# Sums of weight blocks in the second MLP matmul: accumulating DMAs onto a negated copy in place of VectorE subtractions

## The chip, the cores and the metric

The kernel runs on one core of one Trainium2 chip. The metric is the device time of one execution in microseconds. The kernel before took 1455.29 us (median of 3 runs, 1454.57 to 1456.90). Engines are named as in the profile: PE is TensorE, PEld its weight loads, DVE VectorE, ACT ScalarE, POOL GpSimd, SP SyncE. PE, DVE, ACT, POOL and SP each work through a queue of their own in order, and semaphores join them.

## The reference

A two-layer encoder trunk on a sequence of 512 tokens of width 1024, in float32. Layer 0 mixes tokens with dilated window attention, layer 1 with latent attention; after each mixer comes an MLP. The part that matters here is the MLP:

```python
D_MODEL = 1024; SEQ = 512; DEPTH = 2; D_FF = 4 * D_MODEL
def sq_relu_mlp(h, w1, w2):
    a = jax.nn.relu(h @ w1)
    return (a * a) @ w2
...
        h = rms_norm(x, norm_ffn[i])
        x = x + sq_relu_mlp(h, ffn_w1[i], ffn_w2[i])
```

## The kernel before

Every matmul keeps float32 accuracy by splitting both operands in a high and a low part (type fp32r) and adding three products: high x high, high x low, low x high. For weights the split is two instructions: ACT copies the block into a tile `whi`, then DVE subtracts that from the block into `wlo`. Both tile names have four buffers that all weight splits of the kernel use in turn, so a split can run ahead of PE by four half blocks and no more; ACT waits until PE has freed the buffer.

The MLP works through the 4096 hidden columns in four chunks. `up(ch, 0)` and `up(ch, 1)` compute the hidden activations of a chunk with `run_block` (matmuls on line 184, results `acc`, evacuated by ACT on lines 604 and 605). `down` multiplies a chunk by 1024 rows of `w2`, for the first three chunks of each MLP (six times in the program) by `wino`, and for the last chunk by `run_block`. The order is up, up, then for each chunk: up(next, 0), down, up(next, 1).

`wino` is a Strassen-Winograd product on 2 x 2 blocks: seven block products in place of eight. The activations and `w2` are cut in four blocks each; a weight block is two half blocks of 128 partitions x 1024 float32 (512 KB each). The four weight blocks b11, b12, b22, b21 lie in `wqs`, loaded by SP (line 505). The products run in the order 1, 5, 6, 3, 7, 2, 4, 24 matmuls each (line 571), into PSUM tiles `sc` and `tp`, and are added to `resid` on line 553. Their weight operands are, in this order:

- 1: b11
- 5: b12 - b11, written over b11
- 6: b22 minus that, written over b11
- 3: b22
- 7: b22 - b12, written over b12
- 2: b21
- 4: b21 minus the sum of 6, written over b11

`sub` makes these four sums, on line 513, two half blocks each; `split_w` splits each operand into `whi` (line 523) and `wlo` (line 524). A half block may be overwritten by the next sum only when its split is done. `stmp` and `split_a` do the same for the activations (tiles `S` and `asp`).

The program is recorded in the order of the code, and a scheduler then sets the order of each engine's queue by a simulated timeline. It decides where a sum stands relative to the splits and the evacuations.

Of the kernel before, what the change touches and what calls it, by code (L numbers as in the profile page):

```python
# [10 lines left out]
F32 = mybir.dt.float32  # L11
F32R = mybir.dt.float32r
AF = mybir.ActivationFunctionType
ALU = mybir.AluOpType
# [5 lines left out]
NT = S // P  # L20
# [67 lines left out]
def encoder_kernel(ctx: ExitStack, tc: tile.TileContext, x, norm_mix, norm_ffn, a_w_qkv, a_q_gain, a_k_gain,  # L88
                   a_w_o, b_w_in, b_q_a_gain, b_w_qb, b_kv_a_gain, b_w_kvb, b_q_gain, b_k_gain, b_w_o,
                   ffn_w1, ffn_w2, consts, out):  # L90
    nc = tc.nc
    V, A, G, PE = nc.vector, nc.scalar, nc.gpsimd, nc.tensor
    uid = [0]

    def nm(s):
        uid[0] += 1
        return f"{s}_{uid[0]}"
# [42 lines left out]
    def load_raw(src, nk, dims, n):  # L140
        raw = wp.tile([P, 2, 512], F32, tag="raw", name=nm("raw"), bufs=3)
        dst = raw[:, :nk, :n]
        if dims:
            dst = dst.rearrange("p k (t c) -> p k t c", t=dims)
            for k in range(nk):
                nc.sync.dma_start(dst[:, k], src[:, k])
        else:
            nc.sync.dma_start(dst, src)
        return raw

    def load_unit(src, nk, dims, n, key=None, home=None):

        raw = early.pop(key) if key in early else load_raw(src, nk, dims, n)
        if home is None:
            home = [wp.tile([P, 2, 512], F32R, tag=t, name=nm(t)) for t in ("whi", "wlo")]
        hi, lo = home
        A.activation(hi[:, :nk, :n], raw[:, :nk, :n], AF.Copy)  # L157
        V.tensor_tensor(lo[:, :nk, :n], raw[:, :nk, :n], hi[:, :nk, :n].bitcast(F32), op=ALU.subtract)  # L158
        return hi, lo, nk

    def run_block(units, groups, n, mm, evac, outs=NT, name=None, halves=1):

        accs = [acc_p.tile([P, 512], F32, tag="acc", name=nm("acc")) for _ in range(outs)]
        total = sum(u[1] for u in units)
        ui = 0
        kt0 = 0  # L170
        for gi, g in enumerate(groups):
            loaded = []
            for _ in range(g):
                src, nk, dims = units[ui]
                loaded.append(load_unit(src, nk, dims, n, (name, ui)))
                ui += 1
            nkt = 0
            for hv in range(halves):
                for o in range(outs):
                    kt = kt0  # L180
                    for hi, lo, nk in loaded:
                        for j in range(nk):
                            for p_i, (lt, rt, oc) in enumerate(mm(o, kt, hi[:, j], lo[:, j], hv)):
                                PE.matmul(accs[o][:, oc], lhsT=lt, rhs=rt, start=(kt == 0 and p_i == 0 and hv == 0),  # L184
                                          stop=(kt == total - 1 and p_i == 2), skip_group_check=halves > 1)
                            kt += 1
                    nkt = kt
                    if gi == len(groups) - 1 and hv == halves - 1:
                        evac(o, accs[o])
            kt0 = nkt  # L190
# [10 lines left out]
    def w_units(w, n0, n):  # L201

        v = w.rearrange("(k p) c -> p k c", p=P)
        return [(v[:, k:k + 2, n0:n0 + n], 2, None) for k in range(0, v.shape[1], 2)]
# [278 lines left out]
    def split_a(x, pool):  # L483
        t = pool.tile([P, 4, 2, 256], F32R, tag="asp", name=nm("asp"), bufs=4)
        A.activation(t[:, :, 0], x, AF.Copy)
        V.tensor_tensor(t[:, :, 1], x, t[:, :, 0].bitcast(F32), op=ALU.subtract)
        return t

    def wino(tag, Aq, w, wqs, pool, resid):

        v = w.rearrange("(k p) c -> p k c", p=P)
        raw, S = {}, {}

        def load(key, slot):
            ki, ni = key  # L500
            raw[key] = []
            for u in range(2):
                t = wqs[:, 2 * slot + u]
                k0 = 4 * ki + 2 * u
                nc.sync.dma_start(t, v[:, k0:k0 + 2, 512 * ni:512 * ni + 512])
                raw[key].append(t)
        for key, slot in zip(((0, 0), (0, 1), (1, 1), (1, 0)), SLOTS[tag % 2]):
            load(key, slot)
        b11, b12, b22, b21 = raw[0, 0], raw[0, 1], raw[1, 1], raw[1, 0]

        def sub(o, x, y):
            for u in range(2):
                V.tensor_tensor(o[u], x[u], y[u], op=ALU.subtract)  # L513

        def stmp(name, x, y, op):
            if name not in S:
                S[name] = pool.tile([P, 4, 256], F32, tag="S", name=nm("S"), bufs=2)
            V.tensor_tensor(S[name], x, y, op=op)

        def split_w(x):  # L520
            hi = wp.tile([P, 2, 512], F32R, tag="whi", name=nm("whi"))
            lo = wp.tile([P, 2, 512], F32R, tag="wlo", name=nm("wlo"))
            A.activation(hi, x, AF.Copy)  # L523
            V.tensor_tensor(lo, x, hi.bitcast(F32), op=ALU.subtract)  # L524
            return hi, lo

        def operands(p):
            if p == 1:
                return Aq(0, 0), b11
            if p == 5:  # L530
                stmp("c", Aq(1, 0), Aq(1, 1), ALU.add)
                sub(b11, b12, b11)
                return S["c"], b11
            if p == 6:
                stmp("c", S["c"], Aq(0, 0), ALU.subtract)
                sub(b11, b22, b11)
                return S["c"], b11
            if p == 3:
                stmp("c", Aq(0, 1), S["c"], ALU.subtract)
                return S["c"], b22  # L540
            if p == 7:
                stmp("d", Aq(0, 0), Aq(1, 0), ALU.subtract)
                sub(b12, b22, b12)
                return S["d"], b12
            if p == 2:
                return Aq(0, 1), b21
            sub(b11, b21, b11)
            return Aq(1, 1), b11

        def add_to(i, n, banks):  # L550
            for t in range(2):
                sl = resid[:, 2 * i + t, 512 * n:512 * n + 512]
                V.tensor_tensor(sl, sl, banks[t], op=ALU.add)

        banks = {}
        for p, chain, first, adds in ORDER:
            a, wq = operands(p)
            at = split_a(a, pool)
            if first:
                pl, tg = (sc_p, "sc") if chain == "a" else (tp_p, "tp")  # L560
                banks[chain] = [pl.tile([P, 512], F32, tag=tg, name=nm(tg)) for _ in range(2)]
            bk = banks[chain]
            for u in range(2):
                hi, lo = split_w(wq[u])
                for t in range(2):
                    for j in range(2):
                        k = 2 * u + j
                        ah = at[:, k, 0, t * P:(t + 1) * P]
                        al = at[:, k, 1, t * P:(t + 1) * P]
                        for i, (lt, rt) in enumerate(((ah, hi), (ah, lo), (al, hi))):  # L570
                            PE.matmul(bk[t], lhsT=lt, rhs=rt[:, j], start=(first and k == 0 and i == 0),  # L571
                                      stop=(k == 3 and i == 2), skip_group_check=True)
            for i, n in adds:
                add_to(i, n, bk)
# [6 lines left out]
    def mlp(layer, w1, w2, hT_m, resid, pool, done):  # L581
# [4 lines left out]
        def up(ch, grp):  # L586
            if grp == 0:
                if ch % 2:
                    a2s[ch] = pool.tile([P, 8, S], F32, tag="a2", name=nm("a2"))
                else:  # L590
                    a2s[ch] = x16.tile([P, 8, S], F32, tag="x16", name=nm("a2"))
            a2 = a2s[ch]
            c0 = ch * 1024 + grp * 512
            first = c0 == 0

            def mm(o, kt, hi, lo, hv, n=256 if first else 512):
                wh, wl = hi[:, o * P:(o + 1) * P], lo[:, o * P:(o + 1) * P]
                sl = slice(hv * n, hv * n + n)
                hh, hl = hT_m[:, kt, 0, sl], hT_m[:, kt, 1, sl]
                return [(wh, hh, sl), (wh, hl, sl), (wl, hh, sl)]  # L600

            def evac(o, acc):
                f = grp * 4 + o
                A.activation(a2[:, f], acc, AF.Relu)
                A.activation(a2[:, f], a2[:, f], AF.Square)

            run_block(w_units(w1, c0, 512), [4] if first else [1] * 4, 512, mm, evac, halves=2 if first else 1)

        def down(ch):
            a2 = a2s.pop(ch)  # L610
# [3 lines left out]
        def down_last(ch):  # L614
# [13 lines left out]
            for c in range(2):  # L628
                def evac(r, acc, c=c):
# [4 lines left out]
                          mm, evac)  # L634

        up(0, 0)
        up(0, 1)
        for ch in range(3):
            up(ch + 1, 0)
# [316 lines left out]
```

## Time and profile before

| | |
|---|---|
| median of 3 runs | 1455.29 us |
| the profiled execution | 1457.98 us |
| its span, first to last instruction | 1456.2 us |
| granted TensorE clock | 0.995 |
| busy PE / DVE / ACT / POOL | 1422.8 / 903.5 / 710.3 / 117.4 us |
| `sub` on DVE (line 513) | 48 instructions, 58.0 us |
| moved by DMA | 135.58 MB, 93 GB/s mean |

The rows of the profile that the prediction uses stand there. "Busy" is the time in which an engine ran an instruction; a group's row ends in the idle time just before its instructions and what ended it. In a timeline a row is start, duration, engine, line, operation, output<-input and, in brackets, the idle time before it with its releaser. Start times count from the first instruction of the span. A matmul row shows its whole latency, so rows overlap; from one start to the next it is 0.227 us for 128x512.

### The profile page before, as it was taken

The page shows a single profiled execution, that of the slowest core. Times are in us where ns is not written, and L with a number is a line of the kernel's source. Part 1 is how long each engine was busy: PE and PEld are TensorE (multiplying, and loading weights), DVE is VectorE, ACT ScalarE, POOL GpSimd, SP SyncE. Part 2 cuts the span into 40 slices and gives each one's busy share as a digit, 9 for nine tenths or more (in the row PEclk, how much of TensorE's full clock was granted, in tenths as well). Part 3 has the DMA queues.
Part 4 walks back from the last instruction along what each step waited for, and adds up shares of the span by engine and source line. Part 5 has one row for each costly group of instructions (what it writes and reads, how often), then busy time and mean ns, then how long its engine had stood idle before and what let it go on. Part 6 is the DMA issues. An engine that isn't in the chain of part 4 may idle for free.

```text
span 1456.2 us, 19181 instructions
## 1 busy us (share of the span) xinstructions
PE 1422.8 (98%) x7164; PEld 1210.6 (83%) x7164; DVE 903.5 (62%) x1431; ACT 710.3 (49%) x1572; POOL 117.4 (8%) x133
## 2 busy tenths in 40 slices
PE   7999999999999999999999999999999999999998
PEld 6889889889988878888888888776778888888887
DVE  6765466556437655285776835688754286675832
ACT  5544455355335533553644543787633453544530
POOL 1120120011011100000000010322100000000000
PEclk9999999999999999999999999999999999999999
DMA  6325114322531334415151032300014305151031
GB/s 227 102 55 167 59 46 131 102 63 58 171 94 58 95 130 157 147 36 171 40 174 58 15 111 68 97 30 30 30 44 162 127 30 173 44 172 61 7 111 72
DMA packets 113053, 135.58 MB, mean 93 GB/s; under 512 B 7488, under 2 KB 72256, under 8 KB 112960
## 3 DMA queue, kind: packets, MB, share of 16 engines
q1 hardware_dynamic: 112960, 134.35, 29.5%
q8 instruction: 57, 0.93, 0.3%
q14 instruction: 36, 0.29, 0.1%
HBM read 130.13 MB, written 4.19 MB: 92 GB/s over the span
## 4 chain that ended last, share of the span: by engine, by line
PE 94%; ACT 3%; DVE 2%; issue 1%; DMA 0%; POOL 0%; SPq 0%; DVEq 0%; ACTq 0%
PE acc L184 64%; PE sc L571 9%; PE tp L571 7%; PE tp L123 4%; PE acc L867 1%; PE sc L761 1%; PE acc L843 1%; PE sco L440 1%; PE sco L444 1%; PE sc L351 1%; PE sc L843 1%; DVE wlo L158 1%; PE sc L344 0%; PE tp L867 0%; PE sc L340 0%
## 5 line engine op out<-in xcount | busy, mean ns | idle before, releaser
L184 PE MATMUL acc<-whi,hT 128*128 128x512 f32 (+2 forms) x1600 | 486.5, 379 | 5.5 <-DVE t L311 2.2
L158 DVE TENSOR_TENSOR wlo<-raw,whi 128x1024 fp32r<-128x1024 f32 (+3 forms) x186 | 215.3, 1162 | 297.5 <-ACT whi L157 296.5
L157 ACT ACTIVATE whi<-raw 128x1024 fp32r<-128x1024 f32 (+3 forms) x186 | 187.2, 1010 | 317.8 <-PE acc L184 256.6
L184 PEld LDWEIGHTS acc<-whi,hT 128*128 128x128 f32 x1600 | 296.3, 189 | 47.1 <-issue 2.9
L184 PE MATMUL acc<-hT_f,whi 128*128 128x512 f32 (+1 forms) x1152 | 322.7, 367 | 1.7 <-DVE resid L650 1.2
L184 PE MATMUL acc<-wlo,hT 128*128 128x512 f32 (+2 forms) x800 | 299.9, 375 | 0.0
L184 PEld LDWEIGHTS acc<-hT_f,whi 128*128 128x128 f32 x1152 | 209.1, 189 | 37.4 <-DVE resid L650 1.6
L184 PE MATMUL acc<-hT_f,wlo 128*128 128x512 f32 (+1 forms) x576 | 208.3, 366 | 0.0
L184 PEld LDWEIGHTS acc<-wlo,hT 128*128 128x128 f32 x800 | 151.3, 189 | 19.9 <-DVE wlo L158 0.5
L523 ACT ACTIVATE whi<-wqs 128x1024 fp32r<-128x1024 f32 x84 | 89.2, 1062 | 110.2 <-PE sc L571 42.6
L184 PEld LDWEIGHTS acc<-hT_f,wlo 128*128 128x128 f32 x576 | 109.0, 189 | 17.5
L571 PE MATMUL sc<-whi,asp 128*128 128x512 f32 x384 | 122.1, 389 | 0.0
L524 DVE TENSOR_TENSOR wlo<-wqs,whi 128x1024 fp32r<-128x1024 f32 x84 | 102.6, 1222 | 25.9 <-ACT whi L523 25.8
L131 POOL TENSOR_TENSOR qrs<-rs_v,nhalf 128x4 f32<-128x4 f32 x48 | 61.5, 1290 | 408.3 <-DVE rs_v L128 393.8
L571 PE MATMUL tp<-whi,asp 128*128 128x512 f32 x288 | 91.6, 389 | 0.0
L571 PEld LDWEIGHTS sc<-whi,asp 128*128 128x128 f32 x384 | 72.1, 188 | 14.9
L184 PE MATMUL acc<-whi,asp 128*128 128x512 f32 x256 | 78.9, 389 | 0.0
L571 PE MATMUL sc<-wlo,asp 128*128 128x512 f32 x192 | 74.7, 389 | 0.0
L571 PEld LDWEIGHTS tp<-whi,asp 128*128 128x128 f32 x288 | 54.0, 188 | 11.2
L136 ACT ACTIVATE junk<-acc 128x128 f32<-128x128 f32 x192 | 53.0, 276 | 18.9 <-PE acc L184 13.9
L513 DVE TENSOR_TENSOR wqs<-wqs 128x1024 f32<-128x1024 f32 x48 | 58.0, 1219 | 0.2
L184 PEld LDWEIGHTS acc<-whi,asp 128*128 128x128 f32 x256 | 48.1, 188 | 10.0
(191 smaller groups left out, 1895.4 us busy)
## 6 DMA issues: line engine op xcount, KB each, us to landing
raw<-in_ffn_w_dram SPq DMA_DIRECT2D x80, 512.0 KB, 3.7
raw<-in_a_w_qkv_dram SPq DMA_DIRECT2D x96, 256.0 KB, 3.4
wqs<-in_ffn_w_dram SPq DMA_DIRECT2D x48, 512.0 KB, 4.4
raw<-in_a_w_qkv_dram SPq DMA_DIRECT2D x64, 192.0 KB, 2.8
raw<-in_a_w_o_dram SPq DMA_DIRECT2D x8, 512.0 KB, 4.1
raw<-in_b_w_o_dram SPq DMA_DIRECT2D x8, 512.0 KB, 3.7
xt<-in_x_dram SPq DMA_DIRECT2D x8, 256.0 KB, 5.6
vd<-vt SPq DMA_DIRECT2D x8, 256.0 KB, 3.5
```

Of the source, the lines that this page charges most:

```text
L123: PE.transpose(o, i, ident)
L131: G.tensor_tensor(out, v[:, :n], nhalf[:, :n], op=ALU.pow)
L136: A.activation(junk, x, AF.Square, scale=1.0 / math.sqrt(dim), accum_out=out)
L157: A.activation(hi[:, :nk, :n], raw[:, :nk, :n], AF.Copy)
L158: V.tensor_tensor(lo[:, :nk, :n], raw[:, :nk, :n], hi[:, :nk, :n].bitcast(F32), op=ALU.subtract)
L184: PE.matmul(accs[o][:, oc], lhsT=lt, rhs=rt, start=(kt == 0 and p_i == 0 and hv == 0), stop=(kt == total - 1 and p_i == 2), skip_group_che ...
L351: PE.matmul(sc[:, r * P:(r + 1) * P], lhsT=qT[:, r * P:(r + 1) * P], rhs=kT[:, r * P:(r + 1) * P], start=True, stop=True)
L513: V.tensor_tensor(o[u], x[u], y[u], op=ALU.subtract)
L523: A.activation(hi, x, AF.Copy)
L524: V.tensor_tensor(lo, x, hi.bitcast(F32), op=ALU.subtract)
L571: PE.matmul(bk[t], lhsT=lt, rhs=rt[:, j], start=(first and k == 0 and i == 0), stop=(k == 3 and i == 2), skip_group_check=True)
L843: PE.matmul(sc, lhsT=lt, rhs=rt, start=(i == 0), stop=(i == 4))
```

## The change

`sub` no longer subtracts on DVE. ACT writes the negated old block over itself (scale -1.0), and a DMA issued by POOL adds the other block onto it, read again from `w2` in DRAM. So `sub` takes the coordinates of the other block in place of its tile. The second operand in SBUF is no longer read for a sum.

```diff
         def sub(o, x, y):
+
+            ki, ni = x
             for u in range(2):
-                V.tensor_tensor(o[u], x[u], y[u], op=ALU.subtract)
+                k0 = 4 * ki + 2 * u
+                A.activation(o[u], y[u], AF.Copy, scale=-1.0)
+                nc.gpsimd.dma_start(o[u], v[:, k0:k0 + 2, 512 * ni:512 * ni + 512], accum_op=ALU.add)
...
-                sub(b11, b12, b11)
+                sub(b11, (0, 1), b11)
...
-                sub(b11, b22, b11)
+                sub(b11, (1, 1), b11)
...
-                sub(b12, b22, b12)
+                sub(b12, (1, 1), b12)
...
-            sub(b11, b21, b11)
+            sub(b11, (1, 0), b11)
```

`load_unit` and `run_block` also get an argument `by_dma`, which would do the weight split of the other matmuls in the same way; it is False in every call, so these are unchanged. Lines of the changed kernel: the negation is L521, the accumulating DMA L522, `whi` L532, `wlo` L533, the matmuls L580, evacuations L613 and L614.

The scheduler puts the new instructions as follows. First, ACT's queue in the first down projection, before. `whi` 5886 and 5902 are the halves of product 5's operand, 5926 and 5942 those of product 6, 5964 is the first half of product 3; `a` is the evacuation of the up projection.

```order
L523 ACTIVATE whi_5886<-wqs_5335 128x1024
L604 ACTIVATE a_989_5697<-acc_5698 128x512
L605 ACTIVATE a_989_5697<-a_989_5697 128x512
L604 ACTIVATE a_989_5697<-acc_5699 128x512
L605 ACTIVATE a_989_5697<-a_989_5697 128x512
L604 ACTIVATE a_989_5697<-acc_5700 128x512
L605 ACTIVATE a_989_5697<-a_989_5697 128x512
L523 ACTIVATE whi_5902<-wqs_5335 128x1024
L604 ACTIVATE a_989_5697<-acc_5701 128x512
L605 ACTIVATE a_989_5697<-a_989_5697 128x512
L523 ACTIVATE whi_5926<-wqs_5335 128x1024
L523 ACTIVATE whi_5942<-wqs_5335 128x1024
```

The same place of ACT's queue now. Product 5's halves are 5888 and 5904, product 6's 5930 and 5946, product 3's first 5968.

```order
L532 ACTIVATE whi_5888<-wqs_5335 128x1024
L613 ACTIVATE a_989_5697<-acc_5698 128x512
L614 ACTIVATE a_989_5697<-a_989_5697 128x512
L521 ACTIVATE wqs_5335<-wqs_5335 128x1024
L613 ACTIVATE a_989_5697<-acc_5699 128x512
L613 ACTIVATE a_989_5697<-acc_5700 128x512
L614 ACTIVATE a_989_5697<-a_989_5697 128x512 x2
L532 ACTIVATE whi_5904<-wqs_5335 128x1024
L613 ACTIVATE a_989_5697<-acc_5701 128x512
L614 ACTIVATE a_989_5697<-a_989_5697 128x512
L532 ACTIVATE whi_5930<-wqs_5335 128x1024
L521 ACTIVATE wqs_5335<-wqs_5335 128x1024 x2
```

The negation for the first half of product 6 stands behind the first evacuation, and the one for its second half (with the first of product 4) behind the split 5930, which itself waits for a DMA. The split 5946 and then 5968 follow these rows, with one activation split between.

Second, PE's queue where the second half of product 6 begins, now. Before, this half ran whole and product 3 followed it.

```order
L580 MATMUL sc_5841<-whi_5946,asp_5927 128x512
L580 MATMUL sc_5842<-whi_5946,asp_5927 128x512
L580 MATMUL tp_5886<-whi_5968,asp_5965 128x512
L580 MATMUL sc_5841<-wlo_5947,asp_5927 128x512
L580 MATMUL sc_5841<-whi_5946,asp_5927 128x512 x2
```

The first matmul of product 3 (into `tp`) now stands third, ahead of the low part of product 6.

Third, POOL's queue behind the norm ahead of the first MLP, now; the row after the norm's is new, and in each MLP there is one such row.

```order
L131 TENSOR_TENSOR nrs_5220<-rs_v_5218,nhalf 128x1
L131 TENSOR_TENSOR nrs_5267<-rs_v_5265,nhalf 128x1
L131 TENSOR_TENSOR nrs_5314<-rs_v_5312,nhalf 128x1
L522 DMA wqs_5335<-in_ffn_w_dram 128x2x512 x24
L709 TENSOR_TENSOR cgB<-ck,gr 128x4x32
```

All 24 accumulating DMAs of an MLP follow one another there, with none of POOL's other work between. SP's queue is the same before and now.

More of the change, by code (lines that the diff above doesn't have):

```diff
@@ L149, in load_raw, with load_unit @@
         return raw
-    def load_unit(src, nk, dims, n, key=None, home=None):
+    def load_unit(src, nk, dims, n, key=None, home=None, by_dma=False):
         raw = early.pop(key) if key in early else load_raw(src, nk, dims, n)
@@ L157, in load_unit, with run_block @@
         A.activation(hi[:, :nk, :n], raw[:, :nk, :n], AF.Copy)
-        V.tensor_tensor(lo[:, :nk, :n], raw[:, :nk, :n], hi[:, :nk, :n].bitcast(F32), op=ALU.subtract)
+        if by_dma:
+            A.activation(lo[:, :nk, :n], hi[:, :nk, :n].bitcast(F32), AF.Copy, scale=-1.0)
+            nc.gpsimd.dma_start(lo[:, :nk, :n].bitcast(F32), src, accum_op=ALU.add)
+        else:
+            V.tensor_tensor(lo[:, :nk, :n], raw[:, :nk, :n], hi[:, :nk, :n].bitcast(F32), op=ALU.subtract)
         return hi, lo, nk
-    def run_block(units, groups, n, mm, evac, outs=NT, name=None, halves=1):
+    def run_block(units, groups, n, mm, evac, outs=NT, name=None, halves=1, by_dma=False):
         accs = [acc_p.tile([P, 512], F32, tag="acc", name=nm("acc")) for _ in range(outs)]
@@ L174, in run_block @@
                 src, nk, dims = units[ui]
-                loaded.append(load_unit(src, nk, dims, n, (name, ui)))
+                loaded.append(load_unit(src, nk, dims, n, (name, ui), by_dma=by_dma))
                 ui += 1
@@ L605, in evac @@
                 A.activation(a2[:, f], a2[:, f], AF.Square)
-            run_block(w_units(w1, c0, 512), [4] if first else [1] * 4, 512, mm, evac, halves=2 if first else 1)
+            run_block(w_units(w1, c0, 512), [4] if first else [1] * 4, 512, mm, evac, halves=2 if first else 1,
+                      by_dma=False)
         def down(ch):
```

## The prediction

> **What bounds the kernel now.** I read the page first (busy shares, then the chain that ended last), then busy time by stage around the changed code, then PE's waits, and last the instructions of one down projection in order of time.
>
> ```profile
> span 1456.2 us, 19181 instructions
> PE 1422.8 (98%) x7164; PEld 1210.6 (83%) x7164; DVE 903.5 (62%) x1431; ACT 710.3 (49%) x1572; POOL 117.4 (8%) x133
> PE 94%; ACT 3%; DVE 2%; issue 1%; DMA 0%; POOL 0%; SPq 0%; DVEq 0%; ACTq 0%
> ```
>
> TensorE (PE) is busy for 98% of the span and carries 94% of the closing chain. VectorE (DVE), which the change relieves, carries 2%. The changed stage is the six down projections, three in each MLP; the windows are cut to them (busy us of each engine, then clock and DMA share; first, last and sum of six rows).
>
> ```profile
> 638.00:677.00 39.00, 39.00 (x173) 32.28 (x172) 32.56 (x35) 20.50 (x22) 0.00 (x0) 1.00 0.44 135
> ...
> 1348.00:1387.00 39.00, 39.00 (x173) 32.30 (x173) 33.45 (x35) 21.43 (x23) 0.00 (x0) 1.00 0.09 27
> sum 232.00, PE 232.00 PEld 192.07 DVE 195.90 ACT 123.62 POOL 0.00; mean PE 38.67 PEld 32.01 DVE 32.65 ACT 20.60 POOL 0.00
> ```
>
> PE is busy 232.00 of 232.00 us there. DVE is loaded too (195.90), but PE never waits for it. PE's wait list starts with this row, and no row of it has a line of the down projection (L571):
>
> ```profile
> PE tp L123 <- DVE xn L212: 9.0, 1, 9.0
> ```
>
> So work taken from DVE here has nothing to give back. The question is only whether the new path of the weight sums, ACT then DMA, keeps ahead of PE.
>
> **The change, part by part.** Removed: 48 subtractions on DVE. Added: 48 negating copies on ACT (nearest row: an ACT pass over 128x1024 f32, the same size and type) and 48 accumulating DMAs on POOL's queue.
>
> ```profile
> L513 DVE TENSOR_TENSOR wqs<-wqs 128x1024 f32<-128x1024 f32 x48 | 58.0, 1219 | 0.2
> L136 ACT ACTIVATE xn<-resid 128x1024 f32<-128x1024 f32 x12 | 12.7, 1058 | 31.4 <-DVE resid L650 21.0 <-DVE resid L631 10.4
> ```
>
> Removal: 48 x 1.219 = 58 us of DVE; on PE's path, 0. Copies: 48 x 1.06 = 51 us of ACT, 8.5 per projection, beside 20.6 of 38.7 busy; as load they fit (cover: ACT's idle half), as places in ACT's queue they matter, below. POOL does nothing in these windows (0.00), and its next own work is the norm of the next layer, so its 24 DMAs in a row per MLP delay nobody else there. The reread blocks are 48 x 0.5 MB = 24 MB; where the critical ones move, the DMA engines are idle:
>
> ```profile
> 627.00:650.00 23.00, 23.00 (x103) 19.06 (x102) 20.57 (x20) 13.54 (x17) 0.00 (x0) 1.00 0.00 1
> ```
>
> SP's order is the same, and its loads come free no later: two of the blocks lose a reader. Two negations per projection belong to the next one's product 7 and stand in ACT's queue ahead of the second split of product 2, waiting for a block that SP loads after the split of 7.
>
> ```profile
> 653.98 1.22 DVE L524 TENSOR_TENSOR wlo<-wqs,whi 128x1024 fp32r<-128x1024 f32 x1
> 660.44 1.06 ACT L523 ACTIVATE whi<-wqs 128x1024 fp32r<-128x1024 f32 x1 [1.43 <-PE tp L571]
> ```
>
> That split ends at 655.2; plus 4.1 us of load (row below) is 659.3, plus the copy 660.4: just in time for 660.44, and product 2's second half starts on PE only at 668.4 (638.64 + 11 half products of 2.72, less the 0.16 by which the rows of the chain lag). Cost 0.
>
> **The disputed price** is d, from the issue of an accumulating DMA to its data standing in SBUF. No such DMA is in this trace. The nearest rows: the same blocks loaded by SP in this stage, the same over the whole run, a 32 KB transfer, and a POOL instruction against SP's issue.
>
> ```profile
> L505 SPq DMA_DIRECT2D wqs<-in_ffn_w_dram x8: 367/368/368, 650.6 to 668.2; - x8
> DMA to landing us min/median/max: 3.6/4.1/4.4
> ...
> DMA to landing us min/median/max: 3.6/4.4/12.6
> v0c<-vd SPq DMA_DIRECT2D x64, 32.0 KB, 2.2
> L131 POOL TENSOR_TENSOR qrs<-rs_v,nhalf 128x4 f32<-128x4 f32 x48 | 61.5, 1290 | 408.3 <-DVE rs_v L128 393.8 <-DVE stat L360 14.4
> ```
>
> Lower end 3.6: POOL issues as SP does and the addition is free. Upper end 12.6, the slowest landing of these blocks. I take 4.1 for a plain block, plus 2.0 because an addition must also fetch the old block ((4.1 - 2.2) us for 480 KB more, scaled to 512 KB), plus 0.9 because POOL prepares the transfer (1.29 - 0.37): d = 7.0, an estimate, nearest to the 4.1 row.
>
> **What d is covered by.** The first down projection in order of time (product 5 uses the first sum, 6 the second of the same block; a and b are the halves of a block):
>
> ```profile
> 625.04 1.23 DVE L524 TENSOR_TENSOR wlo<-wqs,whi 128x1024 fp32r<-128x1024 f32 x1 [1.24 <-ACT whi L523]
> 633.01 1.06 ACT L523 ACTIVATE whi<-wqs 128x1024 fp32r<-128x1024 f32 x1 [2.24 <-PE acc L184]
> 634.13 1.22 DVE L524 TENSOR_TENSOR wlo<-wqs,whi 128x1024 fp32r<-128x1024 f32 x1
> 635.23 0.63 ACT L605 ACTIVATE a<-a 128x512 f32<-128x512 f32 x1
> 639.56 1.23 DVE L524 TENSOR_TENSOR wlo<-wqs,whi 128x1024 fp32r<-128x1024 f32 x1 [1.95 <-ACT whi L523]
> 641.40 1.06 ACT L523 ACTIVATE whi<-wqs 128x1024 fp32r<-128x1024 f32 x1 [0.72 <-PE sc L571]
> 644.12 1.06 ACT L523 ACTIVATE whi<-wqs 128x1024 fp32r<-128x1024 f32 x1 [1.66 <-PE sc L571]
> 649.52 5.44 PE sc L571 x24
> 652.31 0.39 PE L571 MATMUL sc<-wlo,asp 128*128 128x512 f32 x1
> 652.53 0.61 PE L571 MATMUL sc<-whi,asp 128*128 128x512 f32 x2
> ```
>
> These are: the split of 1a, whi and wlo of 5a, an evacuation, wlo of 5b, whi of 6a, whi of 6b, and of PE product 6 in the chain (5.44 us for 24 matmuls), then its second and third matmul of 6b. The whi starts wait for PE to free a buffer, so DVE's subtraction was hidden. Now, link by link:
> 1. 1a is split at 626.3; negation of 5a until 627.3; landed at 627.3 + d. whi of 5a cannot start before 633.01: covered to d = 5.7.
> 2. 5a is split at 635.35, the evacuation ahead in ACT's queue ends at 635.9, negation of 6a until 636.9, landed at 636.9 + d. Covered by the buffer at 641.40 to d = 4.5; after that ACT stands still at whi of 6a.
> 3. Behind it in ACT's queue stands the negation of 6b, though its input is ready from 640.8. It ends about 2.0 later (two ACT passes), at 638.9 + d, and lands at 638.9 + 2d.
> 4. whi of 6b, then whi of 3a, end at 640.9 + 2d. In the new order PE's third matmul there is the first of 3a, wanted at 652.5. So PE waits once d passes 5.8.
>
> Beyond 5.7 the first link also slides: whi of 5a at 627.3 + d, its split 2.3 later, negation of 6a until 630.7 + d, whi of 6a at 630.7 + 2d, and 3a ready at 634.7 + 3d. PE is late by the larger of 2d - 11.6 and 3d - 17.8: nothing at 5.8, 1.7 at 6.5, 3.2 at 7.0, 6.2 at 8, 9.2 at 9, 12.2 at 10. PE has no slack later to win that back, since it is busy throughout. The sums of product 4 have four products of time, those of 7 a whole projection; they cost nothing.
>
> Sum: six projections x 3.2 = 19.2 us on the profiled execution's 1457.98 (span 1456.2), so 1477.2; that execution lies 2.7 above the median 1455.29, so 1474.5 in the runs' measure.
>
> A rule speaks against this. The Trainium skill, page DMA: Bandwidth & Descriptors, section Anatomy of one DMA, gives a DMA issued by GpSimd 2.0 us plus its bytes at 436 GB/s. For both operands, 1 MB, that would be an estimated 4.4 us, under 5.8, and the time would stay at 1455.3. The 4.1 row of this trace is for half those bytes and a faster issuer, so the trace leans away from it, but holds no DMA of that kind.
>
> **Rivals.** (1) Hidden: d stays under 6.05, the point where six waits reach 2.9 us. Then 1455.3, not slower. It is one mechanism: POOL's preparation overlaps the transfer and the second operand comes with the first. For it: idle DMA engines (0.00) and the quickest landing, 3.6; 3.6 + 2.0 is 5.6, still covered. Against: it needs POOL as quick as SP. The Trainium skill's rule above ends here too. Chance 0.36.
>
> (2) Dear: d over 9.2, because the addition in the DMA engine or the preparation of 256 rows runs far below a copy's rate. At d = 10: 6 x 12.2 = 73, so 1528; at 12.6, 6 x 20 = 120, so 1575. A PE that idles so long may also come back slow; the opening of the trace shows that after 9.03 us of idleness:
>
> ```profile
> 9.03 1.97 PE L123 MATMUL tp<-ck,xn 128*128 128x128 f32 x8 [9.03 <-DVE xn L212]
> 10.98 0.80 PE L184 MATMUL acc<-whi,hT 128*128 128x512 f32 x1
> 16.21 0.72 PE L184 MATMUL acc<-wlo,hT 128*128 128x512 f32 x1
> ```
>
> 0.80 and 0.72 against the 0.39 at 652.31: some 5 us at half pace, 2.6 lost. Six times that is 16 us on top, so 1544 at d = 10. The Trainium skill, page TensorE: Matmul & The Clock Gate, Part 1, puts the drop at about 3.4 us of idleness; by that it would touch my forecast's 3.2 hardly and this rival fully. No wait of that length inside this trace's body tests it. For this rival: 12.6 has been seen. Against: only in a burst of loads. Chance 0.17.
>
> (3) Faster, because a relieved DVE shares memory less with PE. Against: product 6 takes 5.44 us, 0.227 a matmul, and the other five that follow in the chain take the same, in any load of DVE. Under 1452; chance 0.03.
>
> **Numbers.** A change of 0.2% (2.9 us) is about what a measurement of this kernel can tell from none. Forecast, d from 6.05 to 9.2: 0.44, own range 1458 to 1514, likeliest 1474.5. Slower is 0.44 + 0.17 = 0.61, same 0.36, faster 0.03. The range goes from 1454, the hidden case with its scatter, to 1514 (d = 9.2, where PE is 9.8 late: 6 x 9.8 = 59 over the median); it leaves out (2) and (3).
>
> **What would show it.** PE waits that name ACT whi of L532 (6b and 3a) in all six projections, none in the up projections; landing of the accumulating DMA near 7; DVE's busy time down by 58 us, ACT's up by 51. A landing under 5.8 with no PE wait proves (1); waits already at 5a and 6a with slow matmuls behind them, (2). I would be wrong in kind if PE waited at product 4 or 7, or if SP's loads came later.

## The result, and the profile after

The changed kernel took 1477.22 us (median of 4 runs, 1477.16 to 1479.0), the kernel before on the same chip 1455.18 us (4 runs): ratio 1.0152, 95% interval 1.0135 to 1.017. It is slower by 22 us. The profiled execution took 1477.17 us.

The page of the changed kernel first: the span, the busy shares, POOL's DMA queue (packets, MB, share of the 16 DMA engines' time) and the closing chain.

```profile
span 1475.4 us, 19325 instructions
PE 1428.3 (97%) x7164; PEld 1208.6 (82%) x7164; DVE 847.8 (57%) x1383; ACT 750.9 (51%) x1620; POOL 175.3 (12%) x181
q0 software_dynamic: 13056, 25.17, 10.6%
PE 67%; issue 22%; ACT 3%; DMA 3%; POOL 3%; DVE 2%; SPq 0%; POOLq 0%; DVEq 0%; ACTq 0%
```

DVE has lost 55.7 us and ACT gained 40.6 us (the 48 negations have 50.6 us by themselves, but back-to-back instructions overlap a little in ACT's busy time), and the closing chain, which before was PE for 94%, now runs through ACT, POOL and DMA too. The busy time of the six down projections, in windows cut to them (columns as before: PE, PEld, DVE, ACT, POOL, then clock, DMA share, GB/s):

```profile
638.00:680.00 42.00, 39.85 (x167) 32.13 (x166) 28.70 (x32) 22.25 (x23) 6.01 (x5) 0.96 0.76 185
...
1195.00:1237.00 42.00, 40.15 (x176) 32.57 (x175) 29.25 (x32) 23.36 (x25) 6.01 (x5) 1.00 0.75 182
...
sum 251.00, PE 238.39 PEld 192.93 DVE 176.46 ACT 140.25 POOL 31.27; mean PE 39.73 PEld 32.15 DVE 29.41 ACT 23.37 POOL 5.21
```

PE was busy for all of the corresponding windows before; now 12.6 us of them are idle, and the granted clock is 0.96 in five of the six (1.00 in the fourth). PE's list of waits has two rows of the down projection, where it had none; each gives us in total, times and the longest:

```profile
PE sc L580 <- ACT whi L532: 11.8, 6, 2.3
PE tp L580 <- ACT whi L532: 0.7, 3, 0.2
```

The accumulating DMAs by themselves (durations of POOL's instruction, ns, then time from issue to landing):

```profile
L522 POOL DMA_DIRECT2D wqs<-in_ffn_w_dram x48: 1194/1203/1367, 575.2 to 1383.8; - x48
...
DMA to landing us min/median/max: 5.9/6.5/11.4
```

And the first down projection in order of time, ACT's and POOL's rows of the chain (negation, DMA, whi, three times: 5a, 6a, 6b), then PE where the second half of product 6 begins:

```profile
623.08 1.06 ACT L521 ACTIVATE wqs<-wqs 128x1024 f32<-128x1024 f32 x1 [0.34 <-DVE wlo L533]
624.45 1.20 POOL L522 DMA_DIRECT2D wqs<-in_ffn_w_dram  x1 [45.30 <-ACT wqs L521]
630.96 1.06 ACT L532 ACTIVATE whi<-wqs 128x1024 fp32r<-128x1024 f32 x1 [3.19 <-DMA wqs<-in_ffn_w_dram]
633.31 1.06 ACT L521 ACTIVATE wqs<-wqs 128x1024 f32<-128x1024 f32 x1
641.15 1.06 ACT L532 ACTIVATE whi<-wqs 128x1024 fp32r<-128x1024 f32 x1 [2.66 <-DMA wqs<-in_ffn_w_dram]
642.11 1.05 ACT L521 ACTIVATE wqs<-wqs 128x1024 f32<-128x1024 f32 x1
649.85 2.95 ACT L532 ACTIVATE whi<-wqs 128x1024 fp32r<-128x1024 f32 x3 [4.34 <-DMA wqs<-in_ffn_w_dram]
...
648.64 0.39 PE L580 MATMUL sc<-whi,asp 128*128 128x512 f32 x1
650.96 0.73 PE L580 MATMUL sc<-whi,asp 128*128 128x512 f32 x2 [1.93 <-ACT whi L532]
651.90 0.49 PE L580 MATMUL tp<-whi,asp 128*128 128x512 f32 x1 [0.22 <-ACT whi L532]
```

From the end of each negation to the start of the whi that it feeds pass 6.82, 6.78 and 6.69 us: the price d, paid three times in a row, with ACT standing still before each whi (3.19, 2.66, 4.34). At its end PE is 2.1 us late for 6b, and 0.4 more a matmul later.

From the first to the last matmul of a projection (start times in the timeline) it was 37.85 us before, in each of the six; now it is 42.29, 42.34, 41.85, 40.35, 42.29 and 41.77, together 23.8 more. By the gaps between starts, less 0.227 us for each matmul, 15.0 of these are PE standing still ahead of 6b and ahead of the first matmul of 3a; the other 8.8 are matmuls at a slow pace behind it, nearly all in the five projections with the lower clock. (The two spans differ by only 19.2 us, because the profiled execution of before reached its first down projection 3.2 us later, at 638.48 in place of 635.26, and took 1.4 us longer between the two MLPs.)

### The profile page after: what moved, and what is told of

Read it like the earlier page. It is cut to its first block, busy times and chain, and to the rows that moved or that the text cites. A ratio compares the mean times of both kernels' runs of the same rounds, so it can differ in the third digit from the quotient of the medians.

```text
span 1475.4 us, 19325 instructions
## 1 busy us (share of the span) xinstructions
PE 1428.3 (97%) x7164; PEld 1208.6 (82%) x7164; DVE 847.8 (57%) x1383; ACT 750.9 (51%) x1620; POOL 175.3 (12%) x181
## 3 DMA queue, kind: packets, MB, share of 16 engines
q0 software_dynamic: 13056, 25.17, 10.6%
## 4 chain that ended last, share of the span: by engine, by line
PE 67%; issue 22%; ACT 3%; DMA 3%; POOL 3%; DVE 2%; SPq 0%; POOLq 0%; DVEq 0%; ACTq 0%
PE acc L189 50%; PE tp L123 4%; POOL wqs L522 3%; PE sc L580 2%; DMA wqs<-in_ffn_w_dram 2%; PE tp L580 2%; PE acc L877 1%; PE acc L853 1%; PE sc L771 1%; PE sco L449 1%; PE sco L445 1%; PE sc L356 1%; DMA raw<-in_a_w_qkv_dram 1%; PE sc L853 1%; DVE wlo L163 1%
## 5 line engine op out<-in xcount | busy, mean ns | idle before, releaser
L533 DVE TENSOR_TENSOR wlo<-wqs,whi 128x1024 fp32r<-128x1024 f32 x84 | 102.0, 1220 | 116.1 <-ACT whi L532 115.9
L580 PE MATMUL sc<-whi,asp 128*128 128x512 f32 x384 | 128.4, 404 | 11.8 <-ACT whi L532 11.8
L532 ACT ACTIVATE whi<-wqs 128x1024 fp32r<-128x1024 f32 x84 | 87.0, 1054 | 91.7 <-DMA wqs<-in_ffn_w_dram 58.9
L522 POOL DMA_DIRECT2D wqs<-in_ffn_w_dram x48 | 58.0, 1208 | 457.3 <-ACT wqs L521 451.5
L580 PEld LDWEIGHTS sc<-whi,asp 128*128 128x128 f32 x384 | 74.5, 195 | 29.6 <-ACT whi L532 14.4
L580 PE MATMUL tp<-whi,asp 128*128 128x512 f32 x288 | 93.4, 395 | 0.8 <-ACT whi L532 0.7
L580 PE MATMUL sc<-wlo,asp 128*128 128x512 f32 x192 | 77.9, 406 | 0.0
L521 ACT ACTIVATE wqs<-wqs 128x1024 f32<-128x1024 f32 x48 | 50.6, 1055 | 33.2 <-DMA wqs<-in_ffn_w_dram 27.2
L580 PEld LDWEIGHTS tp<-whi,asp 128*128 128x128 f32 x288 | 54.5, 189 | 14.8 <-ACT whi L532 3.7
```

The lines of the kernel that those rows point to most:

```text
L521: A.activation(o[u], y[u], AF.Copy, scale=-1.0)
L522: nc.gpsimd.dma_start(o[u], v[:, k0:k0 + 2, 512 * ni:512 * ni + 512], accum_op=ALU.add)
```

## The experiments

**Which sums cost.** In the first run products 5 and 6 go back to DVE; the second is its complement, with `(5, 6)` in place of `(7, 4)`.

```diff
-        def sub(o, x, y):
+        def sub(o, x, y, p):
...
+                if p not in (7, 4):
+                    V.tensor_tensor(o[u], raw[x][u], y[u], op=ALU.subtract)
+                    continue
                 k0 = 4 * ki + 2 * u
...
```

> The sums of products 7 and 4 stay with the DMA transfers; those of products 5 and 6 go back to VectorE. My theory: only the chain of transfers through products 5 and 6 reaches TensorE, so half the transfers, half the copies on ScalarE and half the issues on POOL cost nothing: 1455 us (1453 to 1458), six projections of 37.9 us each from first to last matmul, no wait of TensorE for a whi of line 535. Rival: the transfers cost by themselves (traffic, ScalarE's copies, POOL's queue), each a share: half of the 22 us, 1466.

> The other half: the sums of products 5 and 6 by DMA transfers, those of 7 and 4 by VectorE. My theory: the whole loss is here, 1477 us (1474 to 1479), with the same wait of 2.0 to 2.7 us ahead of the second half of product 6 and a stretch at half clock behind it. Rival (a share for each transfer): 1466.

Measured: sums of 7 and 4 by DMA 1456.08 us, ratio 1.0001 (0.9992 to 1.001); sums of 5 and 6 by DMA 1477.49 us, ratio 1.0151 (1.0136 to 1.0166). The first has PE busy throughout the stage, as these two windows (first and last projection) show; PE's waits of the second name the same whi (L535 there), in all six projections:

```profile
638.00:677.00 39.00, 39.00 (x174) 32.31 (x173) 31.30 (x34) 22.25 (x23) 2.41 (x2) 1.00 0.67 174
1347.00:1386.00 39.00, 39.00 (x174) 32.31 (x173) 31.50 (x33) 23.34 (x25) 2.41 (x2) 1.00 0.33 66
```

```profile
PE sc L583 <- ACT whi L535: 10.8, 6, 2.0
```

So 24 accumulating DMAs with their traffic, copies and issues cost nothing, and the other 24 cost all of the 22 us. It is where a transfer stands, not that it is there.

**A longer price.** One more POOL operation between negation and DMA:

```diff
                 A.activation(o[u], y[u], AF.Copy, scale=-1.0)
+                G.tensor_scalar(o[u][:, 0, :256], o[u][:, 0, :256], 1.0, None, op0=ALU.mult)
```

> Between each negation and its transfer stands one more operation on POOL (256 of the 1024 elements of a partition, times 1.0), which makes the price d of each sum longer by its own time x, 0.7 to 1.7 us by the nearest rows (738 and 1707 ns for 128 x 256). My theory: three such prices stand in a row ahead of the second half of product 6, so TensorE is later by 3x there in each projection: 1477 + 18x, 1490 at 0.7 and 1508 at 1.7, and still no wait at products 7 and 4. Rival 1: only the last transfer counts, later by x: 1477 + 6x, 1481 to 1487. Rival 2: the loss is not this chain but traffic and copies: 1477.

Measured: 1473.56 us, ratio 1.0126 (1.011 to 1.0142): the added operation and its hand-over took 1.15 us (0.85 and 0.30), and yet the kernel was 3.7 us faster than the changed one. No theory had that. ACT's rows of the first projection show why: negation of 6b, whi of 6a, whi of 6b.

```profile
640.42 1.06 ACT L521 ACTIVATE wqs<-wqs 128x1024 f32<-128x1024 f32 x1
643.68 1.06 ACT L533 ACTIVATE whi<-wqs 128x1024 fp32r<-128x1024 f32 x1 [2.20 <-DMA wqs<-in_ffn_w_dram]
649.15 2.95 ACT L533 ACTIVATE whi<-wqs 128x1024 fp32r<-128x1024 f32 x3 [2.06 <-DMA wqs<-in_ffn_w_dram]
```

The scheduler, with another duration in its simulated timeline, put the negation of 6b ahead of the whi of 6a; in the changed kernel it stands behind (642.11 behind 641.15). The third price no longer waits for the second. What is still lost, 18 us in the six projections, is at full clock in the stage: waits of 1.1 to 1.7 us for 6b, 0.4 us behind each for 3a, and in three projections 1 us at the second half of product 2. The next three runs follow from this.

**The order held, the price longer.** The same POOL operation, with the negation of 6b queued behind the whi of 6a as in the changed kernel:

```diff
+                G.tensor_scalar(o[u][:, 0, :256], o[u][:, 0, :256], 1.0, None, op0=ALU.mult)
...
-                sub(b11, (1, 1), b11)
+                sub(b11, (1, 1), b11, (0,))
...
                 hi, lo = split_w(wq[u])
+                if p == 6 and u == 0:
+                    with tc.issue_after(state["whi"].ins):
+                        sub(b11, (1, 1), b11, (1,))
```

> The run with the added POOL operation again, but with ScalarE's order held as in the changed kernel (neg 6b behind whi 6a), which the first try did not keep. The operation and the hand-over to the transfer were 0.86 + 0.30 us there, so x is 1.15. My theory (three prices in a row): TensorE later by 3.45 us more at product 6 in each projection, 20.7 in all, and the half clock in all six: 1477 + 20.7 + 1 = 1498 us (1493 to 1502). Rival 1 (only the last price counts): 1477 + 6.9 = 1484. Rival 2 (two of the three): 1477 + 13.8 = 1491.

Measured: 1506.78 us, ratio 1.0355 (1.0341 to 1.0369), above my range. The three prices in the first projection, and PE's wait:

```profile
623.41 1.06 ACT L521 ACTIVATE wqs<-wqs 128x1024 f32<-128x1024 f32 x1 [0.34 <-DVE wlo L534]
633.57 1.06 ACT L533 ACTIVATE whi<-wqs 128x1024 fp32r<-128x1024 f32 x1 [5.36 <-DMA wqs<-in_ffn_w_dram]
635.92 1.06 ACT L521 ACTIVATE wqs<-wqs 128x1024 f32<-128x1024 f32 x1
644.52 1.06 ACT L533 ACTIVATE whi<-wqs 128x1024 fp32r<-128x1024 f32 x1 [3.43 <-DMA wqs<-in_ffn_w_dram]
645.49 1.04 ACT L521 ACTIVATE wqs<-wqs 128x1024 f32<-128x1024 f32 x1
654.31 2.95 ACT L533 ACTIVATE whi<-wqs 128x1024 fp32r<-128x1024 f32 x3 [5.88 <-DMA wqs<-in_ffn_w_dram]
...
655.41 1.22 PE L584 MATMUL sc<-whi,asp 128*128 128x512 f32 x2 [5.73 <-ACT whi L533]
```

They are 9.10, 7.54 and 7.78: 24.42 in place of 20.29, 4.13 more (the first one's POOL operation took 1.91 us, not 0.85). Counted from the first matmul of the projection, 6b starts after 19.81 us in place of 15.70, 4.11 later. So the three add up one for one; with one or two of them counting it would have been 1.1 or 1.9. (The gap just ahead of 6b grew by 3.79, from 2.32 to 6.11; 0.3 more is a short wait at 6a.) The six projections take 29.5 us more than in the changed kernel. PE standing still makes 20.5 of these, close to the 20.7 that I expected. What I missed is the clock, for which I had added 1 us: it is at half for 41.0 us here, in place of 17.1, and makes most of the other 9 us (last section).

**The order mended.** All 48 sums by DMA, and one line of order: whi of 6a is queued behind the negation of 6b. The second run also queues the negations for the next projection's product 7 behind the last whi of the projection before, and so out of product 2's way.

```diff
-                hi, lo = split_w(wq[u])
+                hi, lo = split_w(wq[u], state["neg"] if p == 6 and u == 0 else None)
...
+                with tc.issue_after(behind.ins):
+                    A.activation(hi, x, AF.Copy)
...
+                if o is b12 and "end" in state:
+                    with tc.issue_after(state["end"].ins):
+                        last = A.activation(o[u], y[u], AF.Copy, scale=-1.0)
```

> All 48 sums stay with the DMA transfers; only the order on ScalarE is pinned: the negation for the second half of product 6 (neg 6b) stands ahead of the copy whi of the first half (whi 6a), where the changed kernel has it behind. My theory: neg 6b then needs only the split of 5b (whi 5b at 636.3 in the changed kernel, its wlo by about 639), so the last transfer is issued near 640, lands near 646 and the second half is ready ahead of TensorE (648.9): no wait at product 6 and 1455 to 1458 us. A second wait may come to light: the negations of the next projection's product 7, which stand in ScalarE's queue ahead of product 2's whi and wait for SP's load, were covered by less than 0.5 us in the changed kernel (whi 666.0, its first matmul 666.9); without TensorE's lateness they can stop it by 1 to 3 us in four of the six projections: 1460 to 1468. Rival (the transfers themselves are too slow, wherever they are issued): 1474 to 1477.

> As the run with neg 6b ahead of whi 6a, and the negations of the next projection's product 7 pinned behind the last whi of the projection before, so that no whi stands behind one that waits for SP's load. My theory: both places at which a negation's wait stops a whi are gone, all sums still go by DMA, and the time is that before: 1455 to 1458 us, 37.9 us from first to last matmul in each projection. Rival (the transfers cost by themselves where products 5 and 6 follow each other): 1474 to 1477.

Measured: 1457.1 us, ratio 1.0012 (1.0003 to 1.0021), and with both pins 1455.94 us, ratio 1.0001 (0.9992 to 1.0009). The second run's windows of the six projections, their sum:

```profile
sum 234.00, PE 234.00 PEld 193.81 DVE 177.54 ACT 151.31 POOL 35.05; mean PE 39.00 PEld 32.30 DVE 29.59 ACT 25.22 POOL 5.84
```

And ACT's rows of its first projection: negation of 6b, whi of 6a, whi of 6b and 3a.

```profile
640.29 1.06 ACT L525 ACTIVATE wqs<-wqs 128x1024 f32<-128x1024 f32 x1
642.34 1.06 ACT L541 ACTIVATE whi<-wqs 128x1024 fp32r<-128x1024 f32 x1 [0.99 <-DMA wqs<-in_ffn_w_dram]
648.11 2.01 ACT L538 ACTIVATE whi<-wqs 128x1024 fp32r<-128x1024 f32 x2 [2.36 <-DMA wqs<-in_ffn_w_dram]
```

The transfers land no sooner (6.4 us at the median), yet the whole loss is gone: PE is busy 234.00 of 234.00 us and each projection takes 37.85 again. Without the second pin the six projections take 1.6 us more in sum, in steps of 0.3 us and less; ACT stands before the two negations for SP's load there (5.17 us in the second projection). Product 4 starts late in three projections, because DVE's add of product 7's result stands in DVE's queue behind the `wlo` of the late `whi`, and product 2's second half is late by 0.1 and 0.3 us in two. So the second wait is real, but far smaller than the 1 to 3 us that I gave it, because I had misread a row: the matmul at 666.9 is product 2's first, and the whi at 666.0 belongs to its second half, wanted 12 matmuls later (669.6). The mended kernel does not beat the one before, since PE bounds both.

**What makes the price.** The same POOL transfers without the addition, with ACT's order as in the changed kernel:

```diff
-                nc.gpsimd.dma_start(o[u], v[:, ...], accum_op=ALU.add)
+                nc.gpsimd.dma_start(o[u], v[:, ...])
```

> The same POOL transfers, but without the addition (the difference is left out: the second operand is then the one block, not the difference of two). My theory: a plain transfer of the same size lands sooner than the 6.5 us of the accumulating one, near the 4.4 us of SP's loads in the kernel before, d near 4.9 and 3d - 17.8 below nothing: no wait at product 6, 1455 to 1457 us. Rival 1 (POOL's preparation makes the 6.5, the addition is free): landing 6.5, 1477. Between them, landing 5.5 to 6.0 gives d of 5.8 to 6.3 and a wait of 0 to 1.1 us per projection: 1455 to 1462.

Measured: 1456.15 us, ratio 1.0001 (0.9991 to 1.001), no wait of PE in the stage. POOL's queue on its page, then its transfers:

```profile
q0 software_dynamic: 6912, 25.17, 5.3%
```

```profile
L522 POOL DMA_DIRECT2D wqs<-in_ffn_w_dram x48: 722/722/876, 578.1 to 1361.7; - x48
...
DMA to landing us min/median/max: 4.0/4.2/7.7
```

The addition makes the price: 6.5 us to landing with it and 4.2 without (both counted from the start of POOL's instruction, which itself takes 1.20 us against 0.72), nearly twice the packets (13056 against 6912) and twice the DMA engines' time for the same 25.17 MB.

**Is the slow pace the idleness?** Ten matmuls that nothing reads, between the halves of product 6; the second run also pins the negations of the next product 7, as above.

```diff
+                if p == 6 and u == 1:
+                    spare = acc_p.tile([P, 512], F32, tag="acc", name=nm("acc"))
+                    for i in range(10):
+                        PE.matmul(spare, lhsT=at[:, 1, 0, 0:P], rhs=hi[:, 1], start=True, stop=True, ...)
```

> Between the two halves of product 6, TensorE runs ten matmuls more into a spare bank (10 x 227 ns = 2.3 us, nothing reads it), so that it isn't idle while the last transfer is under way. My theory: the half clock of 3.4 us follows from the idle wait; with the wait filled, the second half starts as late as in the changed kernel, but runs at full clock: some 1.7 us less in five projections, and the second short wait is covered too: 1466 to 1470 us, granted clock 1.00 in all six projections. Rival 1: the half clock has another cause (the transfers, the load): 1477, clock 0.96 as now. Rival 2: the wait is not idle time that can be filled, and the matmuls add their own 2.3 us: 1477 + 14 = 1491.

> The ten matmuls between the halves of product 6 again, with the negations of the next projection's product 7 pinned behind the last whi of the projection before, so that the waits at product 2 that the first try had are gone; neg 6b stays behind whi 6a. My theory: what is left in each projection is the chain's own lateness, 2.9 us by the first try's gaps (2493 + 870 less two steps of 227 ns), at full clock in all six: 1456 + 6 x 2.9 = 1473 us (1472 to 1476), that is, some 4 us below the changed kernel, which is late by as much and pays the half clock besides. Rival (the half clock has another cause than TensorE's idleness): 1456 + 6 x 2.9 + 5 x 1.7 = 1482.

Measured: 1486.54 us, ratio 1.0217 (1.0201 to 1.0233) for the first, 1475.74 us, ratio 1.0137 (1.012 to 1.0154), for the second. In both the granted clock is 1.00 in all six projections. The first missed in time, for a reason of its own: PE waited for product 2 as well. ACT's rows there, in the first projection, are a negation for the next projection (standing 6.77 us for SP's load) and, behind it, the whi of product 2's first half, which stands ahead of that negation in the changed kernel; PE waits for it:

```profile
665.43 1.06 ACT L521 ACTIVATE wqs<-wqs 128x1024 f32<-128x1024 f32 x1 [6.77 <-DMA wqs<-in_ffn_w_dram]
666.39 1.04 ACT L532 ACTIVATE whi<-wqs 128x1024 fp32r<-128x1024 f32 x1
...
667.49 0.50 PE L585 MATMUL tp<-whi,asp 128*128 128x512 f32 x1 [0.49 <-ACT whi L532]
```

The pin took 10.8 us off. What is left, 20.0 us above before, is lateness at full clock: the six projections take 247.5 us in sum, against 250.9 in the changed kernel and 227.1 before. So the half clock follows from PE standing still, as the theory said; the rival's 1482 is out. How much of the 22 us it makes the run does not give exactly: it gained 1.5 us by the medians (3.4 us in the six projections) where I expected 4, since product 3's first matmul no longer stands ahead in PE's order, and the second half of 6 starts later (2.8 to 3.1 us in five projections and 4.5 in one, the ten matmuls counted as waiting).

## Why the prediction was right

The forecast was 1474.5 us, slower, in a range of 1454 to 1514; it came to 1477.22.

- PE bounds the stage, so relieving DVE is worth nothing: shown. With both pins DVE and ACT carry the changed load and PE's stage is what it was.
- The copies on ACT, the issues on POOL and the traffic as load cost nothing, shown by the sums of 7 and 4 alone (1.0001) and by the mended kernel.
- The chain, 5a to 6a to 6b with the negation of 6b behind the whi of 6a: shown from both sides, and PE waits where it was said to, at 6b and 3a in the changed kernel, not at product 4 or 7. Lengthened prices add up three times; changing the one queue position takes out nearly all of the loss. The sum behind the formula holds in the trace too: it has 3d + 7.4 us from the end of 5a's negation to the copy of 3a, 27.7 with the measured prices, and the first matmul of 3a starts 27.76 us after that negation ends (651.90 less 624.14).
- The price d, 7.0: 6.5 to landing, 6.76 with the hand-overs. Its terms were off in opposite directions. POOL's preparation, for which I had added 0.9, does not show in the landing (a plain POOL transfer lands in 4.2, SP's in 4.1); the addition, which I put at 2.0, costs 2.3; and the 0.3 us from negation to POOL was missing from the chain. By the formula, 3d - 17.8 is 2.48 at d = 6.76; PE stood still for 15.0 / 6 = 2.5.
- The step that failed is the clock. I had the slow pace after idleness only in rival 2 and wrote that it would touch the forecast's wait hardly. It came after waits of 2.1 to 2.9 us (for 6b and 3a together), in five of six projections, and cost about 1.6 to 2.0 us in each; in the stage it is nearly all of the 8.8 us besides the 15.0 of waiting. That the forecast came so near is luck in part: a wait too long by 0.7 us and a clock left out made up for each other (19.2 forecast; 15.0 + 8.8 found). I wrote that no wait of the length in question tests it in the trace of before, but a shorter one there does. PE waits once for 2.2 us in the window from 91.84 to 95.25 (first row: us in total, times, longest), and the next 3.41 us are at half clock (the figure behind POOL):

```profile
PE acc L184 <- DVE t L311: 2.2, 1, 2.2
```

```profile
91.84:95.25 3.41, 1.46 (x8) 1.49 (x9) 3.41 (x8) 1.15 (x5) 0.00 (x0) 1.00 0.65 184
95.25:98.66 3.41, 3.41 (x13) 3.41 (x12) 3.41 (x7) 0.86 (x5) 1.47 (x1) 0.50 0.54 160
```

- No cost for the negations ahead of product 2: right in the changed kernel, but with far less cover than the 8 us that I read from the trace before. I had written that SP's loads come free no later, and named their coming later as a sign of being wrong in kind. They do come later (three blocks lose a reader, not two, but the split of the block that is loaded over first is itself late): the first for the next projection is issued about 18 us behind the first matmul of the present one in place of 12.1, and they take 7.1 us to landing at the median in place of 4.4. And the whi of 2b starts late, behind the negation, for a matmul at 669.6 (twelve after 2a's first, the PE row). PE, late by itself, did not have to wait for it; with PE on time the same queue cost 1.6 us, until the second pin. The changed kernel's timeline there:

```profile
665.02 1.06 ACT L521 ACTIVATE wqs<-wqs 128x1024 f32<-128x1024 f32 x1 [5.01 <-DMA wqs<-in_ffn_w_dram]
665.98 1.04 ACT L532 ACTIVATE whi<-wqs 128x1024 fp32r<-128x1024 f32 x1
...
666.90 0.39 PE L580 MATMUL tp<-whi,asp 128*128 128x512 f32 x1
```

- Rival 1, hidden: d was above 5.8, so it did not happen; without the addition it did. The Trainium skill, page DMA: Bandwidth & Descriptors, section Anatomy of one DMA, gave by its fit an estimated 4.4 us for both operands; the accumulating transfer measured 6.5, so the estimate does not hold for it. Rival 2: no landing of the critical transfers came near 9.2. Rival 3: a relieved DVE, with PE on time, gave 1.0001, so no gain.

## What to carry to other kernels

A sum moved from an engine to an accumulating DMA trades 1.2 us of that engine for 1.06 us of the one that negates, and adds some 7 us of delay, so it belongs where an operand has several products of time, not in a chain in which each sum is made from the last. Ahead of such a change follow the in-order queue that makes its inputs: one negation behind one copy that waits for a DMA cost 22 us here, and a pin of one queue position brought 20 of them back. A simulated schedule can put that position either way with a small change of some duration, so look it up in the built program, and hold it fixed in experiments.

## What the runs showed of the hardware

The clock falls on a fixed grid. In the changed kernel the half clock begins at 652.73, 738.07, 823.40, 1294.44 and 1379.77 us, and the distances are whole multiples (25, 25, 138, 25) of 3.413 us. Windows of that grid, first PE's busy time, then the granted clock behind DVE, ACT and POOL: of the changed kernel the one with the wait and the next in the first projection, then the same in the fourth, which kept full clock.

```profile
649.32:652.73 3.41, 1.56 (x5) 0.96 (x6) 1.79 (x2) 2.88 (x4) 0.00 (x0) 1.00 0.75 138
652.73:656.14 3.41, 3.41 (x9) 2.66 (x9) 3.41 (x5) 2.92 (x4) 1.14 (x1) 0.50 0.47 129
1205.70:1209.11 3.41, 1.92 (x9) 1.26 (x7) 0.01 (x1) 0.97 (x2) 0.00 (x0) 1.00 1.13 202
1209.11:1212.52 3.41, 3.05 (x12) 2.16 (x13) 3.29 (x4) 3.41 (x5) 0.00 (x0) 1.00 0.25 46
```

The wait of the fourth projection lies across a boundary of the grid, and neither window is idle enough. The run with the lengthened price and the order held shows two slow windows after one long wait:

```profile
649.70:653.11 3.41, 0.00 (x0) 0.00 (x0) 0.23 (x1) 0.00 (x0) 1.55 (x2) 1.00 0.95 139
653.11:656.52 3.41, 1.10 (x3) 0.66 (x3) 1.13 (x1) 2.21 (x3) 0.00 (x0) 0.50 0.95 169
656.52:659.94 3.42, 3.42 (x9) 2.65 (x9) 3.42 (x4) 3.42 (x4) 0.69 (x1) 0.50 0.21 55
```

Counting a matmul as 227 ns from its start, every full-clock window of the two MLPs (behind their first few us, in which the norm and narrower matmuls mix), in all eleven traces of this case, in which PE stood idle for 2.09 us or more is followed by one at half clock, and none with 2.07 us or less is. Whether the same limit holds for matmuls of other widths is not shown. So a wait of 2 us can bring 3.4 us at half pace, or none, by where it falls, as in the fourth projection. The Trainium skill, page TensorE: Matmul & The Clock Gate, Part 1, gives a free-running window of 3413 ns, and the trace agrees (3.413); it puts the drop behind an idle window, and here 2.1 idle us of the 3.4 were enough.

The other surprise is the accumulating DMA: it lands 2.3 us later than the plain one, and POOL's instruction for it takes 0.5 us longer, for the same bytes from DRAM.
